# Mean of the last tokens ahead of the last quarter of the columns, by a column of summed weights in the last projection

## The chip, the cores and the metric

The kernel runs on one core of one Trainium2 chip. Five engines work side by side and are held together by semaphores: PE (TensorE, matrix products, with its weight load PEld), DVE (VectorE), ACT (ScalarE), POOL (GpSimd) and SP (SyncE), whose queue issues every DMA of this kernel. The metric is the device time of one execution in microseconds, lower is better; times are compared as medians of several runs.

## The reference

Two gated attention layers with a LayerNorm behind each, on 256 tokens of 1024 features. What matters here is the end of the second layer: the gated attention output `o * silu(gate)` is projected by `moba_w_o`, a scaled residual is added, and each token (a row) is normalized over its 1024 columns.

```
def layer_norm(x, g, b):
    xf = x.astype(jnp.float32)
    mu = jnp.mean(xf, axis=-1, keepdims=True)
    var = jnp.mean(jnp.square(xf - mu), axis=-1, keepdims=True)
    return ((xf - mu) * lax.rsqrt(var + LN_EPS) * g + b).astype(x.dtype)
...
def moba_mixer(x, k_blocks, v_blocks, k_mean, w_in, w_o, cos, sin):
...
    return (o * jax.nn.silu(gate)) @ w_o
...
        x = layer_norm(ALPHA * x + y, ln_g[layer], ln_b[layer])
    return x
```

The mean `mu` of a row is needed before the first subtraction, the variance before the multiplication by its inverse root.

## The kernel before

Tokens stand in two tiles of 128 (tok 0 and tok 1), features in eight chunks of 128. Every product of two float32 matrices is done in three matmuls: each operand is split into a high part in the reduced type fp32r and a low part, the rest (`split`: ACT casts the high part at line 376, DVE or POOL subtracts it from the source at line 387), and `passes` (line 406 in the profile) multiplies high by high, high by low and low by high into one PSUM bank.

Weights come in units of 128 x 1024, one DMA each, in the order of a list. A unit lands in one of five `raw` buffers, and its two parts go into one of six `wh` and six `wl` buffers; the last two units of the projections `oa`, `vb` and `ob` go into `x_h` and `x_l` instead. So the weights of the last projection, `ob`, eight units of one feature chunk by all 1024 columns, are split while the second attention layer still runs.

`token_products` runs a projection of tokens: for tok 0, one unit after the other over the columns 0 to 511 and 512 to 1023; tok 1 follows eight units later. With `last` given (only for `ob`), tok 1 goes through the eight units three times, for the columns 0 to 511, 512 to 767 and 768 to 1023, each in a PSUM bank of its own, and `last_b` is called when a bank is complete. It adds the scaled residual (`m` in the profile, `x1[1]` in the code), takes `bn_stats` of each 256 columns (line 918), and, after the last quarter, joins them with `bn_aggr` to mean and variance (line 924, in `mv`). POOL raises the variance to the power -0.5 (line 387, `mv<-mv,mhalf`). Then there are two steps for each quarter of 256 columns, both at line 391: the first, `act_h<-m,mv,lng`, subtracts the mean and multiplies by the gain, the second, `act_h<-act_h,mv,lnb`, multiplies by the inverse root and adds the bias; `act_h` is here the output row. Three DMAs write the output of tok 1.

The first layer's normalization (`layer_norm`, lines 807 and 808) is done for tok 0 and tok 1 in turn, on tiles of 512 columns; its result `m` is transposed by PE (line 420, `pt`), split into `act_h` and `act_l`, and projected by `vb`.

In the second attention layer, per head pair: scores into the banks `s`, DVE masks them and takes the minimum (line 713), ACT exponentiates and sums (line 380, `e`), DVE takes the reciprocal (line 719), POOL or DVE scales (line 400), PE transposes (`pt`), ACT copies the transposed tile (line 376), PE multiplies by the values (`pv`). Meanwhile PE computes projections of gates, queries and keys for later heads as filler.

The order of instructions on each engine isn't the order of the code: `Schedule` collects all operations with an estimated duration and their dependencies, and emits them by a priority list over the five engines. An engine takes its instructions strictly in the order in which they were emitted.

Of the kernel before, what the change touches and what calls it, by code (L numbers as in the profile page):

```python
# [8 lines left out]
F32R = mybir.dt.float32r  # L9
# [4 lines left out]
P = 128  # L14
# [329 lines left out]
def trunk(ctx, tc, W0, xtok, W, gq, gkv, lng, lnb, cosa, sina, coska, sinka, cosb, sinb, maskd, identd, out):  # L344
# [93 lines left out]
    raws = {}  # L438

# [14 lines left out]
    def weights(name, k):  # L454
        u = U[name, k]
        while state["hl"] <= u:
# [5 lines left out]
            if nm == "kr":  # L462
                hl = sc.val(wp, [P, 1024], F32R, "wh", HL_BUFS).rearrange("p (a b c) -> p a b c", b=2, c=64)
                r = raws.pop(v)[:, 0:n].rearrange("p (a c) -> p a c", c=64)
                split(hl[:, :, 0, :].at(0), hl[:, :, 1, :].at(1), r, n)
                hls[v] = hl.rearrange("p a b c -> p a (b c)")
                state["hl"] += 1
                continue
            if nm in ("oa", "vb", "ob") and kk >= 6:
                if kk == 6:  # L470
                    extra["h"] = C([P, 2, 1024], "x_h", F32R)
                    extra["l"] = C([P, 2, 1024], "x_l", F32R)
# [48 lines left out]
    def token_products(name, nk, lhs, tags, lag, done, last=None):  # L521
        banks = [None, None]
        n1 = nk * (3 if last else 1)
        for i in range(max(nk, n1 + lag)):
            for tok in range(2):
# [8 lines left out]
                if tok and last:  # L534
                    parts = (((0, 512), (512, 768), (768, 1024))[j // nk],)
                for c0, c1 in parts:
                    h, l = wsl(w, c0, c1)
                    ah, al = lhs(k, tok)
                    o = banks[tok][j // nk if tok and last else c0 // 512][:, 0:c1 - c0]
                    passes(o, ah, al, h, l, k == 0, k == nk - 1, c1 - c0)  # L540
                if tok and last:
                    if k == nk - 1:
                        last(o, c0, c1)
# [368 lines left out]
    st4, mv4 = C([P, 4, 6], "bst4"), C([P, 4], "mv4")  # L912

    def last_b(o, c0, c1):
        z = x1[1]
        stt(z[:, c0:c1].at(c0), z[:, c0:c1].at(None), ALPHA, o, ALU.mult, ALU.add, c1 - c0)
# [5 lines left out]
        if c1 < D:  # L922
            return
        sc.op("dve", 80, lambda: nc.vector.bn_aggr(A(mv4[:, 0:2]), A(st4)), [st4], [mv4.at(0)])
        tt(mv4[:, 2:3].at(1), mv4[:, 1:2].at(0), mhalf, ALU.pow, 5, "pool")
        y = C([P, 2, D], "act_h")[:, 0]

        def step(a, b, one):
            zi, yo = z[:, a:b].at(max(k for k in (0, 512, 768) if k <= a)), y[:, a:b].at(a // S)
            if one:  # L930
                stt(yo, zi, mv4[:, 0:1].at(0), gb[:, a:b], ALU.subtract, ALU.mult, b - a)
            else:
                stt(yo, yo, mv4[:, 2:3].at(1), bb[:, a:b], ALU.mult, ALU.add, b - a)

        for q in range(3):
            step(q * S, q * S + S, True)
        for q in range(2):
            step(q * S, q * S + S, False)
        dma(out[1][:, 0:512], y[:, 0:512], 2048 * P, r=[y.at(0), y.at(1)])
        step(768, 1024, True)  # L940
        for q in (2, 3):
            step(q * S, q * S + S, False)
            dma(out[1][:, q * S:q * S + S], y[:, q * S:q * S + S], 1024 * P, r=[y.at(q)])
# [94 lines left out]
```

## Time and profile before

| | us |
|---|---|
| median of three runs | 282.68 |
| lowest and highest run | 281.94 and 285.47 |
| the profiled execution | 284.01 |
| its span, first to last instruction | 282.2 |

The profiled execution has 1.81 us around its span, and stands 1.33 us above the median. Its TensorE clock was granted at 0.979 on average; it is 1.00 from 222 to 256 us. Times below are counted from the start of the span. In a row of the timeline stand the start, the duration, the engine, the line, the operation, its output and inputs with their shapes, the number of instructions merged in the row, and in brackets the idle time ahead of it with what ended it. SPq is the queue of SP. Duration means from start to end of one instruction; on ACT and DVE the next one can start some 0.1 us before the end of the one in front of it where it needn't wait for it.

### The profile page before, as it was taken

The numbers are of one execution on the slowest core, as the hardware profiler recorded it, in microseconds if no ns is written. First come the engines' busy times: TensorE is split into PE (matmuls) and PEld (weight loads), VectorE is DVE, ScalarE is ACT, GpSimd is POOL, SyncE is SP. The second block draws the span as 40 slices with busy tenths as digits, with TensorE's granted clock in tenths as the row PEclk, the third lists the DMA queues.
The fourth block names the chain that finished last, engine by engine and source line by source line (L and its number), as shares of the span: only waits on it lengthen the run. The fifth ranks groups of instructions, "written<-read, shape, count | busy, mean of one in ns | idle before, by whom it ended". The sixth has DMA issues, their size and how long they took to land.

```text
span 282.2 us, 5363 instructions
## 1 busy us (share of the span) xinstructions
PE 269.2 (95%) x1948; PEld 246.6 (87%) x1948; DVE 209.0 (74%) x450; ACT 159.6 (57%) x330; POOL 57.0 (20%) x72
## 2 busy tenths in 40 slices
PE   7799989999999999999999999999999999999990
PEld 4799989989989999878877889999999999887880
DVE  2557779989988767655998546868988979685655
ACT  3537769567695768822505744546855858692000
POOL 2000042400040034201010000522324445421100
PEclk9599999999999999999999999999999999999996
DMA  7897865766262442262288784465848768430012
GB/s 266 271 328 271 291 222 181 272 224 217 89 215 75 153 149 75 77 223 74 81 293 268 291 282 165 148 209 161 296 119 322 204 224 310 104 113 2 0 74 74
DMA packets 18537, 52.31 MB, mean 185 GB/s; under 512 B 2896, under 2 KB 6096, under 8 KB 18512
## 3 DMA queue, kind: packets, MB, share of 16 engines
q1 hardware_dynamic: 18512, 51.98, 54.8%
q8 instruction: 15, 0.25, 0.3%
q14 instruction: 10, 0.08, 0.1%
HBM read 45.68 MB, written 1.05 MB: 166 GB/s over the span
## 4 chain that ended last, share of the span: by engine, by line
PE 79%; issue 12%; DVE 5%; ACT 1%; POOL 1%; DMA 0%; SPq 0%; DVEq 0%; ACTq 0%
PE proj L406 58%; PE s L406 11%; PE pv L406 6%; PE pt L420 4%; DVE wl L387 2%; DVE m L391 1%; DVE act_h L391 1%; ACT wh L376 1%; DVE bst L807 0%; DMA raw<-in_W 0%; POOL mv L387 0%; POOL rk L387 0%; SPq L368 0%; DVE act_l L387 0%; ACT act_h L376 0%
## 5 line engine op out<-in xcount | busy, mean ns | idle before, releaser
L387 DVE TENSOR_TENSOR wl<-raw,wh 128x1024 fp32r<-128x1024 f32 (+2 forms) x74 | 87.2, 1187 | 22.0 <-ACT wh L376 20.3
L376 ACT CAST wh<-raw 128x1024 fp32r<-128x1024 f32 (+2 forms) x75 | 74.7, 1003 | 33.8 <-PE proj L406 14.9
L406 PE MATMUL proj<-act_h,wh 128*128 128x256 f32 x280 | 79.1, 283 | 0.0
L406 PE MATMUL proj<-act_h,wl 128*128 128x256 f32 x280 | 78.2, 279 | 0.0
L406 PE MATMUL proj<-act_l,wh 128*128 128x256 f32 x280 | 78.2, 279 | 0.0
L406 PEld LDWEIGHTS proj<-act_l,wh 128*128 128x128 f32 x280 | 52.6, 188 | 0.0
L406 PEld LDWEIGHTS proj<-act_h,wh 128*128 128x128 f32 x280 | 52.6, 188 | 0.0
L406 PEld LDWEIGHTS proj<-act_h,wl 128*128 128x128 f32 x280 | 52.5, 188 | 0.0
L380 ACT ACTIVATE e<-e,st 128x256 f32<-128x256 f32 x64 | 28.6, 451 | 8.0 <-DVE st L713 7.7
L400 POOL TENSOR_SCALAR e<-e,st 128x256 f32<-128x256 f32 (+1 forms) x32 | 16.1, 520 | 48.8 <-DVE st L719 48.7
L406 PE MATMUL s<-kq 128*128 128x256 f32 (+1 forms) x100 | 18.9, 316 | 0.4 <-DVE wl L387 0.4
L406 PE MATMUL proj<-x_h,wh 128*128 128x256 f32 x64 | 18.5, 289 | 0.0
L406 PE MATMUL proj<-x_h,wl 128*128 128x256 f32 x64 | 17.9, 279 | 0.0
L406 PE MATMUL proj<-x_l,wh 128*128 128x256 f32 x64 | 17.9, 279 | 0.0
L387 DVE TENSOR_TENSOR x_l<-raw,x_h 128x256 fp32r<-128x256 f32 (+1 forms) x14 | 10.4, 764 | 9.7 <-ACT x_h L376 9.7
L406 PEld LDWEIGHTS s<-kq 128*128 128x128 f32 x100 | 15.6, 190 | 1.9 <-PE pt L420 0.6
L376 ACT COPY pt<-pt 128x384 f32<-128x384 f32 x32 | 14.9, 474 | 3.5 <-PE pt L420 3.4
L376 ACT CAST x_h<-raw 128x256 fp32r<-128x256 f32 (+1 forms) x14 | 9.5, 685 | 11.3 <-DMA raw<-in_W 11.3
L420 PE MATMUL pt<-ident,e 128*128 128x128 f32 x96 | 15.1, 275 | 0.0
L387 POOL TENSOR_TENSOR t<-t,t512b 128x512 f32<-128x512 f32 x5 | 6.9, 1371 | 31.6 <-DVE t512b L387 17.5
L713 DVE CUSTOM_DVE_ANT_0 e<-s,masks,sca 128x256 f32<-128x256 f32 (+1 forms) x32 | 11.9, 412 | 1.8 <-PE pt L420 0.7
L387 POOL TENSOR_TENSOR mv<-mv,mhalf 128x1 f32<-128x1 f32 x4 | 3.5, 871 | 44.5 <-DVE mv L398 36.2
(166 smaller groups left out, 577.3 us busy)
## 6 DMA issues: line engine op xcount, KB each, us to landing
raw<-in_W SPq DMA_DIRECT2D x66, 512.0 KB, 4.3
raw<-in_W SPq DMA_DIRECT2D x7, 640.0 KB, 7.8
kq<-x_h SPq DMA_DIRECT2D x24, 96.0 KB, 2.2
raw<-in_W SPq DMA_DIRECT2D x5, 384.0 KB, 3.9
kq<-x_h SPq DMA_DIRECT2D x24, 64.0 KB, 2.0
lng<-in_lng SPq DMA_DIRECT2D x2, 512.0 KB, 4.1
lnb<-in_lnb SPq DMA_DIRECT2D x2, 512.0 KB, 5.3
raw<-in_xtok SPq DMA_DIRECT2D x2, 512.0 KB, 3.5
```

What stands on the lines that cost most here:

```text
L376: nc.scalar.copy(A(o), A(i))
L380: nc.scalar.activation(A(o), A(i), func, bias=A(bias), scale=A(scale), accum_out=A(accum))
L387: sc.op(eng, dur, lambda: e.tensor_tensor(A(o), A(a), A(b), op=op), [a, b], [o], lock=not (is_ps(a) or is_ps(b)))
L391: sc.op("dve", dur, lambda: nc.vector.scalar_tensor_tensor(A(o), A(a), A(s), A(b), op0=op0, op1=op1), [a, s, b], [o], lock=not (is_ps(a) o ...
L400: fn = lambda: e.tensor_scalar(A(o), A(a), A(s1), s2, op0=op0, op1=op1)
L406: nc.tensor.matmul(A(out_), A(lt), A(rh), start=st, stop=sp_, skip_group_check=True)
L420: nc.tensor.transpose(A(x), A(y), A(ident))
L713: nc.vector.tensor_tensor_reduce(A(e[:, cs]), A(ps[:, cs]), A(msk), scale=A(scale[b]), scalar=3.0e38, op0=ALU.add, op1=ALU.min, accum_out= ...
```

## The change

A product's mean over the columns is the product with the mean over the columns of the weights. The change uses this for the last quarter of `ob`. For each of the eight `ob` units, ACT sums the columns 768 to 1023 of the raw weights (one pass over 256 columns with an accumulator, into `wsum`), and the sum is split into a high and a low part, too, and written twice, as two extra columns behind the third quarter. For that, a unit's parts are kept as four quarters at a distance of 272 columns in buffers of 1088 columns. The second of the three turns of tok 1 is 258 columns wide instead of 256, so that its bank holds, in column 256, the sum over the last quarter of the projection before that quarter is computed.

The residual's part of the sum, `ms[:, 0:1]`, is taken by one more accumulating pass of ACT over `x1[1]` when the first layer's normalization has produced it. When the second bank is complete, the mean of the whole row is put together in `ms[:, 3:4]` from `bn_aggr` of three quarters and these sums, and the first step of the three quarters 0 to 2 is emitted there, ahead of the last bank. Behind the last bank stand `bn_stats`, `bn_aggr` of all four quarters (for the variance), the power on POOL, the first step of the last quarter and the second step of all four. The three DMAs of the output are the same in size; the first follows the second quarter.

The core of the diff:

```
+    wsum = C([P, 8], "wsum")
...
-                h = sc.val(wp, [P, 1024], F32R, "wh", HL_BUFS)[:, :]
-                l = sc.val(wp, [P, 1024], F32R, "wl", HL_BUFS)[:, :]
+                h = sc.val(wp, [P, 1088], F32R, "wh", HL_BUFS)[:, :]
+                l = sc.val(wp, [P, 1088], F32R, "wl", HL_BUFS)[:, :]
             r = raws.pop(v)
+            if nm == "ob":
+
+                h, l = (t.at((kk, 0)).rearrange("p (a b) -> p a b", b=272) for t in (h, l))
+                split(h[:, :, 0:S], l[:, :, 0:S], r[:, 0:n].at(0).rearrange("p (a b) -> p a b", b=S), n, eng=on("w", nm, kk))
+                act(T([P, S], "scr", 1), r[:, 768:n].at(0), S, AF.Identity, accum=wsum[:, kk:kk + 1].at(kk))
+                split(h[:, 2, S:S + 2], l[:, 2, S:S + 2], wsum[:, kk:kk + 1].at(kk).bc([P, 2]), 2)
+                hls[v] = (h, l, kk, "ob")
+                state["hl"] += 1
+                continue
...
+        if early == "ob":
+            if c1 - c0 == S + 2:
+                return h[:, c0 // S, 0:S + 2], l[:, c0 // S, 0:S + 2]
+            return h[:, c0 // S:c1 // S, 0:S], l[:, c0 // S:c1 // S, 0:S]
...
-                    parts = (((0, 512), (512, 768), (768, 1024))[j // nk],)
+                    parts = (((0, 512), (512, 770), (768, 1024))[j // nk],)
...
-    st4, mv4 = C([P, 4, 6], "bst4"), C([P, 4], "mv4")
-
-    def last_b(o, c0, c1):
+    st4, mv4, ms = C([P, 4, 6], "bst4"), C([P, 4], "mv4"), C([P, 4], "ms")
+    act(T([P, S], "scr", 1), x1[1][:, 768:D].at(None), S, AF.Identity, scale=ALPHA / D, accum=ms[:, 0:1].at(0))
+    y = C([P, 2, D], "act_h")[:, 0]
+
+    def last_b(bk, c0, c1):
         z = x1[1]
-        stt(z[:, c0:c1].at(c0), z[:, c0:c1].at(None), ALPHA, o, ALU.mult, ALU.add, c1 - c0)
...
+        stt(z[:, c0:c1].at(c0), z[:, c0:c1].at(None), ALPHA, bk[:, 0:c1 - c0], ALU.mult, ALU.add, c1 - c0)
+        if c0 == 512:
+            stt(ms[:, 1:2].at(1), bk[:, S:S + 1], 1.0 / D, ms[:, 0:1].at(0), ALU.mult, ALU.add, 1)
...
+        elif c0 == 512:
+            sc.op("dve", 80, lambda: nc.vector.bn_aggr(A(mv4[:, 0:2]), A(st4[:, 0:3, :])), [st4.at(q) for q in range(3)], [mv4.at(0)])
+            stt(ms[:, 3:4].at(3), mv4[:, 0:1].at(0), 0.75, ms[:, 1:2].at(1), ALU.mult, ALU.add, 1)
+            for q in range(3):
+                step(q * S, q * S + S, True)
+        else:
+            sc.op("dve", 80, lambda: nc.vector.bn_aggr(A(mv4[:, 0:2]), A(st4)), [st4], [mv4.at(0)])
+            tt(mv4[:, 2:3].at(1), mv4[:, 1:2].at(0), mhalf, ALU.pow, 5, "pool")
+            step(768, 1024, True)
+            for q in range(4):
+                step(q * S, q * S + S, False)
+                if q:
+                    a = 0 if q == 1 else q * S
+                    dma(out[1][:, a:q * S + S], y[:, a:q * S + S], (q * S + S - a) * 4 * P, r=[y.at(i) for i in range(a // S, q + 1)])
```

What this does to the order is seen at three places. The first is the end of DVE's queue, where `s` and the later `proj` are the second and third bank of tok 1, `m_1733` is its row and `bst`, `mv` hold its statistics. Before:

```order
L391 SCALAR_TENSOR_TENSOR m_1733<-m_1733,s 128x256
L918 BN_STATS bst_3329<-m_1733 128x6
L391 SCALAR_TENSOR_TENSOR m_1733<-m_1733,proj 128x256
L918 BN_STATS bst_3329<-m_1733 128x6
L924 BN_AGGR mv_3371<-bst_3329 128x2
L391 SCALAR_TENSOR_TENSOR act_h<-m_1733,mv_3371,lng 128x256 x3
L391 SCALAR_TENSOR_TENSOR act_h<-act_h,mv_3371,lnb 128x256 x2
L391 SCALAR_TENSOR_TENSOR act_h<-m_1733,mv_3371,lng 128x256
L391 SCALAR_TENSOR_TENSOR act_h<-act_h,mv_3371,lnb 128x256 x2
```

The same place on DVE after the change, with `ms` for the sums and the mean:

```order
L391 SCALAR_TENSOR_TENSOR m_1733<-m_1733,s 128x256
L391 SCALAR_TENSOR_TENSOR ms<-s,ms 128x1
L946 BN_STATS bst_3365<-m_1733 128x6
L951 BN_AGGR mv_3391<-bst_3365 128x2
L391 SCALAR_TENSOR_TENSOR ms<-mv_3391,ms 128x1
L391 SCALAR_TENSOR_TENSOR act_h<-m_1733,ms,lng 128x256 x3
L391 SCALAR_TENSOR_TENSOR m_1733<-m_1733,proj 128x256
L946 BN_STATS bst_3365<-m_1733 128x6
L956 BN_AGGR mv_3391<-bst_3365 128x2
L391 SCALAR_TENSOR_TENSOR act_h<-m_1733,ms,lng 128x256
L391 SCALAR_TENSOR_TENSOR act_h<-act_h,mv_3391,lnb 128x256 x4
```

Three of the four first steps moved from behind the third bank to ahead of it, with three small instructions new in front of them.

The second place is ACT's queue where the first layer's tok 1 has been normalized: the two `act_h` rows are the casts of its two transposed halves, and the `wh` row between them is a weight unit of the projection `vb`.

```order
 L376 CAST wh<-raw 128x1024
 L376 CAST act_h<-pt 128x4x128
+L380 ACTIVATE scr,ms<-m_1733 128x256
 L376 CAST wh<-raw 128x1024
 L376 CAST act_h<-pt 128x4x128
```

The pass over the residual was put between the first half's cast and the weight unit's.

The third place is ACT's queue in the second attention layer, at the casts of the gated attention output `oa` of two head pairs and the exponentials of the next two tiles of scores (the four `e,st` rows). Before:

```order
L376 CAST big_h<-oa 128x256 x2
L376 COPY pt<-pt 128x384
L380 ACTIVATE e,st<-e,st 128x256
L380 ACTIVATE e,st<-e,st 128x128
L380 ACTIVATE e,st<-e,st 128x256
L380 ACTIVATE e,st<-e,st 128x128
L378 ACTIVATE t_3002<-proj 128x256
L376 CAST wh<-raw 128x1024
```

The same place on ACT after the change:

```order
L376 CAST big_h<-oa 128x256 x2
L376 COPY pt<-pt 128x384
L380 ACTIVATE scr,wsum<-raw 128x256 x2
L380 ACTIVATE e,st<-e,st 128x256
L380 ACTIVATE e,st<-e,st 128x128
L380 ACTIVATE e,st<-e,st 128x256
L380 ACTIVATE e,st<-e,st 128x128
L378 ACTIVATE t_3018<-proj 128x256
L376 CAST wh<-raw 128x4x256
L376 CAST wh<-wsum 128x2
```

Two passes over weights stand ahead of the exponentials, and a cast of two columns behind the unit's cast. PE's order changes only here: the transposes of the second of these two tiles stand 3 instead of 9 filler matmuls behind the next scores, the scores after that move behind `pv`, and the transposes and scores behind them trade places with a few filler matmuls. SP and POOL keep their order.

More of the change, by code (lines that the diff above doesn't have):

```diff
@@ L462, in weights @@
             if nm == "kr":
-                hl = sc.val(wp, [P, 1024], F32R, "wh", HL_BUFS).rearrange("p (a b c) -> p a b c", b=2, c=64)
+                hl = sc.val(wp, [P, 1088], F32R, "wh", HL_BUFS)[:, 0:1024].rearrange("p (a b c) -> p a b c", b=2, c=64)
                 r = raws.pop(v)[:, 0:n].rearrange("p (a c) -> p a c", c=64)
@@ L539, in token_products @@
                     o = banks[tok][j // nk if tok and last else c0 // 512][:, 0:c1 - c0]
+                    if last and (c1 - c0) % S == 0:
+                        o = o.rearrange("p (a b) -> p a b", b=S)
                     passes(o, ah, al, h, l, k == 0, k == nk - 1, c1 - c0)
@@ L542, in token_products @@
                     if k == nk - 1:
-                        last(o, c0, c1)
+                        last(banks[tok][j // nk], c0, c1 // S * S)
                 elif j == nk - 1:
@@ L909, in finish_b, with step @@
             dma(out[tok][:, cs], x1[tok][:, cs].at(hf), 2048 * P)
-    st4, mv4 = C([P, 4, 6], "bst4"), C([P, 4], "mv4")
-    def last_b(o, c0, c1):
+    st4, mv4, ms = C([P, 4, 6], "bst4"), C([P, 4], "mv4"), C([P, 4], "ms")
+    act(T([P, S], "scr", 1), x1[1][:, 768:D].at(None), S, AF.Identity, scale=ALPHA / D, accum=ms[:, 0:1].at(0))
+    y = C([P, 2, D], "act_h")[:, 0]
+    def last_b(bk, c0, c1):
         z = x1[1]
-        stt(z[:, c0:c1].at(c0), z[:, c0:c1].at(None), ALPHA, o, ALU.mult, ALU.add, c1 - c0)
+        def step(a, b, one):
+            zi, yo = z[:, a:b].at(max(k for k in (0, 512, 768) if k <= a)), y[:, a:b].at(a // S)
+            if one:
+                stt(yo, zi, ms[:, 3:4].at(3), gb[:, a:b], ALU.subtract, ALU.mult, b - a)
+            else:
+                stt(yo, yo, mv4[:, 2:3].at(1), bb[:, a:b], ALU.mult, ALU.add, b - a)
+        stt(z[:, c0:c1].at(c0), z[:, c0:c1].at(None), ALPHA, bk[:, 0:c1 - c0], ALU.mult, ALU.add, c1 - c0)
+        if c0 == 512:
+            stt(ms[:, 1:2].at(1), bk[:, S:S + 1], 1.0 / D, ms[:, 0:1].at(0), ALU.mult, ALU.add, 1)
         for q in range(c0 // S, c1 // S):
@@ L921, in last_b @@
             ts(st4[:, 0, 2:3].at(0), st4[:, 0, 2:3].at(0), D * LN_EPS, None, ALU.add, None, 1, "dve")
[L922 to L943, printed above, removed]
+        elif c0 == 512:
[3 more added lines that the diff above has]
+                step(q * S, q * S + S, True)
+        else:
+            sc.op("dve", 80, lambda: nc.vector.bn_aggr(A(mv4[:, 0:2]), A(st4)), [st4], [mv4.at(0)])
[6 more added lines that the diff above has]
+                    dma(out[1][:, a:q * S + S], y[:, a:q * S + S], (q * S + S - a) * 4 * P, r=[y.at(i) for i in range(a // S, q + 1)])
     token_products("ob", 8, lhs_of(ogh2, ogl2), (("proj", "proj"), ("s", "s", "proj")), LAG, finish_b, last_b)
```

4 lines of the change are left out of this document (2 added, 2 removed).

## The prediction

> **What bounds the kernel now.** I read the page's busy shares first, then the timeline of the end, then the waits around each place where the order puts new instructions.
>
> ```profile
> span 282.2 us, 5363 instructions
> PE 269.2 (95%) x1948; PEld 246.6 (87%) x1948; DVE 209.0 (74%) x450; ACT 159.6 (57%) x330; POOL 57.0 (20%) x72
> ```
>
> PE is busy for 95% of the span, so a gain can only come from where PE isn't working: the end. A loss comes from whatever makes PE wait. The timeline from the last matmul on:
>
> ```profile
> 274.31 0.28 PE L406 MATMUL proj<-x_h,big_l 128*128 128x256 f32 x1
> 274.63 0.42 DVE L391 SCALAR_TENSOR_TENSOR m<-m,proj 128x256 f32<-128x256 f32 x1 [1.96 <-PE proj L406]
> 275.09 0.43 DVE L918 BATCH_NORM_STATS2 bst<-m 128x6 f32<-128x256 f32 x1
> 275.55 0.27 DVE L924 BATCH_NORM_AGGREGATE mv<-bst 128x2 f32<-128x24 f32 x1
> 275.85 1.30 DVE L391 SCALAR_TENSOR_TENSOR act_h<-m,mv,lng 128x256 f32<-128x256 f32 x3
> 275.89 0.56 POOL L387 TENSOR_TENSOR mv<-mv,mhalf 128x1 f32<-128x1 f32 x1 [8.32 <-DVE mv L924]
> 277.07 0.87 DVE L391 SCALAR_TENSOR_TENSOR act_h<-act_h,mv,lnb 128x256 f32<-128x256 f32 x2
> 277.86 0.47 DVE L391 SCALAR_TENSOR_TENSOR act_h<-m,mv,lng 128x256 f32<-128x256 f32 x1
> 278.26 0.87 DVE L391 SCALAR_TENSOR_TENSOR act_h<-act_h,mv,lnb 128x256 f32<-128x256 f32 x2
> ...
> L368 SPq DMA_DIRECT2D out<-act_h x3: 332/333/405, 278.0 to 279.2; - x3
> ...
> out<-act_h SPq DMA_DIRECT2D x2, 128.0 KB, 1.9
> ```
>
> From 274.63 on DVE is never idle: residual, statistics, eight steps, done at 279.13. The last DMA is issued at 279.2, lands 1.9 us later, and the span ends at 282.2. Before 274.63 DVE sat idle for 1.96 us. Every step taken out of this queue is worth its pitch; POOL's power ends at 276.45 and nobody waits for it, because three first steps cover it.
>
> **The end, part by part.** Removed behind the third bank: three first steps. `bn_aggr` still ends at 275.82. The remaining first step no longer needs it, so it starts as a DVE instruction without a wait does, about 0.08 early (277.86 against 277.94), at 275.75, and ends at 276.22. Now the power loses its cover: the second steps wait for it. Its price has two rows, 0.56 above and this one, from the first layer's normalization:
>
> ```profile
> 144.89 0.74 DVE L391 SCALAR_TENSOR_TENSOR m<-m,mv,lng 128x512 f32<-128x512 f32 x1
> 145.05 1.00 POOL L387 TENSOR_TENSOR mv<-mv,mhalf 128x1 f32<-128x1 f32 x1 [11.38 <-DVE mv L398]
> 146.09 0.75 DVE L391 SCALAR_TENSOR_TENSOR m<-m,mv,lnb 128x512 f32<-128x512 f32 x1 [0.46 <-POOL mv L387]
> ```
>
> There the power began 0.16 behind the start of a DVE step, took 1.00, and ended 0.42 behind that step's end (146.05 against 145.63); in the old end it began 0.04 behind one and took 0.56. In the new end it begins at 275.89, 0.14 behind, so I take the slow form: 276.22 + 0.42 = 276.64, and DVE 0.04 later, 276.68. Four second steps follow: 3 x 0.40 + 0.47 = 1.67, done at 278.35 instead of 279.13, a gain of 0.78. With the fast form (276.45) it is 0.97. [...]
>
> The three DMAs are ready at 277.55, 277.95 and 278.35. At 0.33 to 0.41 per issue SP keeps up, so the last goes out 0.78 earlier, too. They come a little closer together, which I cost at nothing (bounds 0 and 0.3, from spreads of 1.2 before and 0.8 after): the landing of 1.9 covers the others' transfer.
>
> **Ahead of the third bank.** The moved work must fit before 274.63.
>
> ```profile
> 271.79 0.42 DVE L391 SCALAR_TENSOR_TENSOR m<-m,s 128x256 f32<-128x256 f32 x1 [1.20 <-PE s L406]
> 272.25 0.43 DVE L918 BATCH_NORM_STATS2 bst<-m 128x6 f32<-128x256 f32 x1
> ...
> L398 DVE TENSOR_SCALAR mv<-mv 128x1 f32<-128x1 f32 x3 | 0.5, 154 | 0.1
> ```
>
> Residual until 272.21, one column of `ms` (0.15, nearest row `mv`) until about 272.3, statistics until 272.75, `bn_aggr` 0.27, `ms` 0.15, three first steps 1.30, with hand-overs of 0.03: done between 274.5 and 274.6. It fits with about 0.1 to spare, so it costs 0; if the small ones cost double, 0.3 of the gain goes.
>
> PE's second turn is two columns wider: 24 matmuls at a pitch of 0.117 for 256 columns (274.31 is 0.117 behind its predecessor) give 24 x 2/256 x 0.117 = 0.02. The 72 matmuls of 512 columns now read the weights from two stretches instead of one. The nearest row is the scores', whose third matmul reads two stretches of keys:
>
> ```profile
> 244.59 0.52 PE L406 MATMUL s<-kq 128*128 128x256 f32 x3
> 244.94 0.28 PE L406 MATMUL proj<-act_h,wh 128*128 128x256 f32 x1
> ```
>
> Three in 0.35 is the plain pitch of 0.117, so I take 0; a hundredth for three, the rows' resolution, times 72 would be 0.2, the upper bound.
>
> **The pass over the residual, at 149 us.** This is the term that the diff hides. ACT, DVE and PE there:
>
> ```profile
> 148.37 0.59 ACT L376 CAST act_h<-pt 128x512 fp32r<-128x512 f32 x1 [7.05 <-PE pt L420]
> 148.85 1.05 ACT L376 CAST wh<-raw 128x1024 fp32r<-128x1024 f32 x1
> ...
> 149.80 0.59 ACT L376 CAST act_h<-pt 128x512 fp32r<-128x512 f32 x1
> ...
> 149.94 1.22 DVE L387 TENSOR_TENSOR wl<-raw,wh 128x1024 fp32r<-128x1024 f32 x1
> ...
> 151.08 0.68 DVE L387 TENSOR_TENSOR act_l<-pt,act_h 128x512 fp32r<-128x512 f32 x1
> ...
> 151.68 2.35 DVE L387 TENSOR_TENSOR x_l<-raw,x_h 128x1024 fp32r<-128x1024 f32 x2
> ...
> 153.08 0.39 PE L406 MATMUL proj<-x_l,act_h 128*128 128x512 f32 x1
> ```
>
> The `wl` at 149.94 waits for the cast that ends at 149.90; `act_l` and two `x_l` follow without a gap. The first `x_l` ends at 152.90, and PE reads it at 153.08: only 0.13 to spare with a hand-over of 0.05. The new pass goes ahead of the cast. What it takes is seen in the exponentials, the same form:
>
> ```profile
> 222.17 0.51 ACT L380 ACTIVATE e<-e,st 128x256 f32<-128x256 f32 x1
> 222.59 0.19 ACT L380 ACTIVATION_READ_ACCUMULATOR e<-e,st 128x1 f32 x1
> 222.68 0.39 ACT L380 ACTIVATE e<-e,st 128x128 f32<-128x128 f32 x1
> ```
>
> From 222.17 to 222.68, 0.51. So the cast, `wl`, `act_l` and `x_l` come 0.51 later, and PE waits 0.51 - 0.13 = 0.38. PE has no later idle time of its own from which to take it back (it computes in order, and what it waits for in the next layer hangs on its own results), so I charge all of it. Bounds: 0, if the order's slack is larger than these rows say, and 0.51. [...]
>
> **The passes over the weights.** Eight passes at 0.51, eight two-column casts (nearest row below), eight two-column subtractions on DVE (0.15 as `mv`, 1.2 together, in its idle time).
>
> ```profile
> L378 ACT ACTIVATE sca<-proj,eps 128x2 f32<-128x2 f32 x1 | 0.3, 256 | 0.0
> ...
> 236.40:256.40 20.00, 19.60 (x145) 17.55 (x144) 15.91 (x53) 15.09 (x42) 6.87 (x10) 1.00 0.41 115
> ...
> 237.27 0.51 ACT L380 ACTIVATE e<-e,st 128x256 f32<-128x256 f32 x1 [0.41 <-DVE st L713]
> ...
> 238.63 3.52 POOL L400 TENSOR_SCALAR e<-e,st 128x256 f32<-128x256 f32 x4 [1.33 <-DVE st L719]
> ...
> 242.06 0.59 PE L406 MATMUL s<-kq 128*128 128x256 f32 x3 [0.40 <-DVE wl L387]
> 242.49 0.28 PE L406 MATMUL proj<-act_h,wh 128*128 128x256 f32 x1
> ```
>
> From 236.40 to 256.40 ACT is busy for 15.09 of 20 us (the fourth busy time of the row); six passes and some six casts, 6 x 0.51 + 6 x 0.26 = 4.6, go there, nearly all of the 4.9 idle. Two passes stand ahead of the exponentials at 237.27. With 0.41 idle there and 1.02 new, these come about 0.5 later (two passes from 236.76). POOL's scaling, done at 242.15, would be done at about 242.7. The transposes that need it now stand three filler matmuls behind the scores: 242.49 + 3 x 0.12 = 242.85. It just fits, by 0.1. Behind it I followed each transposition and each copy in the new order in the same way and found 0.6 or more to spare. So I cost this at nothing; the cover is the filler matmuls, and if it is gone, each tile late by 0.5 costs PE up to that. Bounds 0 and 1.0, two such delays.
>
> **Sum.** -0.78 + 0.02 + 0.38 = -0.38. On the profiled execution, 284.01 (1.81 around its span of 282.2), that gives 283.6, span 281.8. That execution is 1.33 above the median of the runs; from the median, 282.68, the forecast is 282.3.
>
> **Rivals.** First, the whole gain: PE doesn't wait at 153, or wins it back. For it: the spare of 0.13 is a difference of rows that vary by some hundredths; against it: DVE's four instructions stand back to back. It gives 282.68 - 0.76 = 281.9, and 281.7 with the fast power.
>
> Second, slower: ACT becomes the bound of the second attention layer. One mechanism: the passes at 236.8 delay exponentials, the scaling and so the transposes at 242.85. It decides once PE waits more than 0.38 there; the price is 1.0 at full, 283.3. For it: 4.6 us put into 4.9 idle. Against it: PE's filler.
>
> Third, the change doesn't do what it says: the moved steps aren't through at 274.63 (the chain of small instructions costs 0.3 each instead of 0.15) and hold the residual of the last bank up, and the DMAs' bunching takes 0.3. Then 0.6 of the gain goes, 282.9. Against it: the small rows are 0.15 each time.
>
> **How the numbers follow.** Forecast 0.45, first rival 0.2, second 0.2, third 0.1, none of these 0.05. The range takes in all three rivals, from 281.7 less some 0.4 for the runs' scatter (their lowest is 0.7 below the median) to 283.3 and 0.4: 281.3 to 283.7. 2%, about what a measurement of this kernel can tell from no change, is 5.7 us; no case comes near. Faster by that 0.01, slower 0.02, the rest within.
>
> **What would show it.** In the changed profile: three first steps ending by 274.6 + 0.4 with DVE idle or just free at the last residual; between the last matmul's end and the last `lnb` 0.8 less than 4.5; POOL's power at about 0.75 (0.56 is the fast form); PE with an idle of 0.3 to 0.4 at `proj<-x_l` near 153.5, released by DVE `x_l`; and between 236 and 258 no wait of PE above 0.5. Wrong would be: waits of PE on POOL `e` or ACT `pt` there, or a wider pitch of the matmuls that read the weights in quarters.

## The result, and the profile after

| | kernel before | changed kernel |
|---|---|---|
| median, first session (22 runs each) | 283.0 | 285.62 |
| lowest and highest | 279.51 and 285.47 | 282.21 and 289.66 |
| ratio, 95% interval | | 1.0107 (1.0081 to 1.0133) |
| ratio in a second session (12 runs against 29) | | 1.0049 (1.0022 to 1.0076) |
| profiled execution, its span | 284.01, 282.2 | 283.29, 281.1 |

Medians are over all runs, while the ratios leave out, on both sides, runs more than 1.5% above the fastest of the same kernel. The changed kernel is slower by 0.5 to 1.1%, 1.6 to 2.6 us, and not 0.4 us faster. The three runs of before that the prediction started from stood low: over all sessions the medians of the kernel before lie between 283.0 and 284.3.

The two profiled executions can't be compared by their spans. These are the page's rows of the granted clock, before and then after, in 40 slices of some 7 us:

```profile
PEclk9599999999999999999999999999999999999996
```

```profile
PEclk9999999999999999999999999999999999999997
```

Before had the clock at half (0.50) for 6.8 us near its start: from 8.80 us on, the starts of 24 matmuls spread over 5.81 us there, and those of the same 24 over 3.21 in after, which had the clock in full (1.00) until its matmuls were done. Such half windows stand ahead of the last matmul in 12 of the 20 profiles of this study, at changing places. So below I compare stretches between two matmuls with the same place in PE's order; where a half window lies in between, the text says so.

The end, in the timeline of the changed kernel:

```profile
272.79 1.27 DVE L391 SCALAR_TENSOR_TENSOR act_h<-m,ms,lng 128x256 f32<-128x256 f32 x3
274.24 0.42 DVE L391 SCALAR_TENSOR_TENSOR m<-m,proj 128x256 f32<-128x256 f32 x1 [0.18 <-PE proj L406]
274.70 0.43 DVE L946 BATCH_NORM_STATS2 bst<-m 128x6 f32<-128x256 f32 x1
275.16 0.26 DVE L956 BATCH_NORM_AGGREGATE mv<-bst 128x2 f32<-128x24 f32 x1
275.34 0.42 DVE L391 SCALAR_TENSOR_TENSOR act_h<-m,ms,lng 128x256 f32<-128x256 f32 x1
275.50 0.67 POOL L387 TENSOR_TENSOR mv<-mv,mhalf 128x1 f32<-128x1 f32 x1 [8.33 <-DVE mv L956]
276.20 1.67 DVE L391 SCALAR_TENSOR_TENSOR act_h<-act_h,mv,lnb 128x256 f32<-128x256 f32 x4 [0.45 <-POOL mv L387]
277.11 1.31 SPq L368 DMA_DIRECT2D out<-act_h  x3
```

The three first steps end at 274.06, 0.18 us ahead of the last residual: the moved work fits. Behind it stand one first step, 0.45 us of idle while DVE waits for POOL's power (0.67), and four second steps, which end at 277.87. From the start of the last matmul to the end of the span it is 7.18 us; before it was 7.88. The gain of the end is there: 0.70. On DVE alone it is 0.87 (from the last residual's start to the last step's end 3.63 us instead of 4.50); the rest goes behind the last step, where the last of the three DMAs, now closer together, is issued some 0.1 later and takes some 0.1 more to land.

The pass over the residual, at 146 us, ACT and PE:

```profile
146.15 0.42 ACT L380 ACTIVATE scr<-m 128x256 f32<-128x256 f32 x1
146.47 0.19 ACT L380 ACTIVATION_READ_ACCUMULATOR scr<-m 128x1 f32 x1
146.56 1.04 ACT L376 CAST wh<-raw 128x1024 fp32r<-128x1024 f32 x1
...
150.27 0.40 PE L406 MATMUL proj<-x_h,act_h 128*128 128x512 f32 x1
150.65 0.50 PE L406 MATMUL proj<-x_l,act_h 128*128 128x512 f32 x1
150.98 0.40 PE L406 MATMUL proj<-x_h,act_l 128*128 128x512 f32 x1
```

From pass to cast it is 0.41 us. The first matmul with `x_l` starts 0.38 behind the one with `x_h`, where the pitch is 0.23: a wait of 0.15, and 0.33 instead of 0.23 once more behind it.

The attention of the second layer, around the transposes that wait longest. Changed kernel, timelines of POOL, DVE and PE:

```profile
241.43 0.55 PE L420 MATMUL pt<-ident,e 128*128 128x128 f32 x3 [0.31 <-POOL e L400]
...
247.24 1.88 POOL L400 TENSOR_SCALAR e<-e,st 128x256 f32<-128x256 f32 x2 [2.30 <-DVE st L735]
247.74 1.22 DVE L387 TENSOR_TENSOR wl<-raw,wh 128x1024 fp32r<-128x1024 f32 x1
249.17 0.55 PE L420 MATMUL pt<-ident,e 128*128 128x128 f32 x3 [0.59 <-POOL e L400]
```

Before, the same places:

```profile
246.24 1.22 DVE L387 TENSOR_TENSOR wl<-raw,wh 128x1024 fp32r<-128x1024 f32 x1
247.70 0.83 POOL L400 TENSOR_SCALAR e<-e,st 128x256 f32<-128x256 f32 x2 [2.03 <-DVE st L719]
249.00 0.49 PE L420 MATMUL pt<-ident,e 128*128 128x128 f32 x3
```

In the changed order DVE's low part of a weight unit (`wl`, 1.22) starts in the middle of POOL's two scalings, and they take 1.88 instead of 0.83; PE waits 0.59. Before, `wl` was over at 247.46, and the scaling began at 247.70. The kernel before has the slow form elsewhere: the four scalings of 3.52 from 238.63 on, which the prediction shows, would be 1.66 at this pace, and on DVE two `wl` run beside them:

```profile
238.37 1.21 DVE L387 TENSOR_TENSOR wl<-raw,wh 128x1024 fp32r<-128x1024 f32 x1
...
240.67 1.25 DVE L387 TENSOR_TENSOR wl<-raw,wh 128x1024 fp32r<-128x1024 f32 x1 [0.51 <-ACT wh L376]
```

The wait at 241.43 is the one that the prediction held covered by 0.1.

Last, a row far from anything that the diff touches: the 280 matmuls of 256 columns with `act_l` and `wh`, from the pages of before and after (total, mean ns of one):

```profile
L406 PE MATMUL proj<-act_l,wh 128*128 128x256 f32 x280 | 78.2, 279 | 0.0
```

```profile
L406 PE MATMUL proj<-act_l,wh 128*128 128x256 f32 x280 | 79.1, 283 | 0.0
```

One takes 4 ns longer, in stages that begin over 100 us ahead of the change's first instruction (146.15). With its two sister groups these are 840 matmuls.

### The profile page after: what moved, and what is told of

It reads as the page before. It is cut to its first block, busy times and chain, and to the rows that moved or that the text cites. A ratio compares the mean times of both kernels' runs of the same rounds, so it can differ in the third digit from the quotient of the medians.

```text
span 281.1 us, 5393 instructions
## 1 busy us (share of the span) xinstructions
PE 269.2 (96%) x1948; PEld 246.7 (88%) x1948; DVE 210.1 (75%) x461; ACT 163.8 (58%) x356; POOL 57.0 (20%) x72
## 3 DMA queue, kind: packets, MB, share of 16 engines
HBM read 45.68 MB, written 1.05 MB: 166 GB/s over the span
## 4 chain that ended last, share of the span: by engine, by line
PE 74%; issue 14%; DVE 5%; POOL 3%; ACT 1%; DMA 0%; SPq 0%; POOLq 0%; DVEq 0%; ACTq 0%
PE proj L406 56%; PE s L406 8%; PE pv L406 6%; PE pt L420 4%; POOL e L400 2%; DVE wl L387 2%; DVE m L391 1%; DVE bst L823 1%; POOL mv L387 1%; DVE act_h L391 0%; ACT wh L376 0%; DMA raw<-in_W 0%; ACT e L380 0%; POOL rk L387 0%; SPq L368 0%
## 5 line engine op out<-in xcount | busy, mean ns | idle before, releaser
L406 PE MATMUL proj<-act_h,wh 128*128 128x256 f32 x280 | 80.1, 286 | 0.0
L406 PE MATMUL proj<-act_h,wl 128*128 128x256 f32 x280 | 79.1, 283 | 0.0
L406 PE MATMUL proj<-act_l,wh 128*128 128x256 f32 x280 | 79.1, 283 | 0.0
L406 PEld LDWEIGHTS proj<-act_l,wh 128*128 128x128 f32 x280 | 53.6, 191 | 0.0
L406 PEld LDWEIGHTS proj<-act_h,wh 128*128 128x128 f32 x280 | 53.5, 191 | 0.0
L406 PEld LDWEIGHTS proj<-act_h,wl 128*128 128x128 f32 x280 | 53.5, 191 | 0.0
L400 POOL TENSOR_SCALAR e<-e,st 128x256 f32<-128x256 f32 (+1 forms) x32 | 17.1, 548 | 50.0 <-DVE st L735 48.1
L420 PEld LDWEIGHTS pt<-ident,e 128*128 128x128 f32 x96 | 11.1, 140 | 2.5 <-POOL e L400 1.5
```

The lines of the kernel that those rows point to most:

```text
L400: fn = lambda: e.tensor_scalar(A(o), A(a), A(s1), s2, op0=op0, op1=op1)
L406: nc.tensor.matmul(A(out_), A(lt), A(rh), start=st, stop=sp_, skip_group_check=True)
L420: nc.tensor.transpose(A(x), A(y), A(ident))
```

## Experiments

Each kernel ran against the kernel before on the same chip. The following table gives what I read from the traces: the time from the start of one matmul to another's, counted by place in PE's order. A: 741 matmuls of the first layer, from about 39 us on. B: the next 46, with the first layer's last `x_l`. C: the next 300. D: from the scores near 224 us to the start of the last matmul. E: from there to the end of the span. F: time around the span, median over the runs.

| kernel | A | B | C | D | E | F | ratio (95% interval) |
|---|---|---|---|---|---|---|---|
| before | 104.52 | 10.46 | 40.17 | 49.50 | 7.88 | 1.79 | |
| before, run again | 104.50 | 10.46 | 40.17 | 50.10 | 7.87 | 1.80 | 0.9983 (0.9950 to 1.0017) |
| wide1088 | 104.50 | 10.46 | 40.17 | 50.43 | 7.89 | 1.80 | 0.9985 (0.9954 to 1.0016) |
| before_plus32 | 104.89 | 10.48 | 39.94 | 50.02 | 7.87 | 1.80 | 0.9986 (0.9954 to 1.0019) |
| before_plus64 | 104.99 | 10.52 | 40.55 | 49.91 | 7.87 | 1.79 | 1.0020 (0.9975 to 1.0066) |
| before_plus96 | 104.73 | 10.47 | 40.33 | 50.56 | 7.88 | 1.78 | 1.0027 (0.9982 to 1.0071) |
| code_on_dve | 104.52 | 10.46 | 40.18 | 50.55 | 7.86 | 1.78 | 0.9946 (0.9905 to 0.9987) |
| code_on_act | 104.44 | 10.48 | 40.19 | 49.36 | 7.87 | 1.77 | 0.9973 (0.9928 to 1.0018) |
| tail_only | 104.50 | 10.47 | 40.17 | 50.54 | 7.18 | 1.77 | 1.0009 (0.9971 to 1.0047) |
| changed | 104.97 | 10.80 | 40.54 | 50.72 | 7.18 | 2.16 | 1.0107 (1.0081 to 1.0133) |
| changed, run again | 104.97 | 10.79 | 40.55 | 51.52 | 7.18 | 2.12 | 1.0049 (1.0022 to 1.0076) |
| sums_mean_late | 104.97 | 10.79 | 40.55 | 50.96 | 7.88 | 2.01 | 1.0121 (1.0076 to 1.0167) |
| after_pad128 | 103.93 | 10.83 | 40.09 | (51.82) | 7.18 | 2.15 | 1.0005 (0.9963 to 1.0046) |
| after_residual_late | 103.89 | 10.55 | 40.09 | (53.66) | 7.19 | 2.14 | 1.0088 (1.0042 to 1.0133) |
| passes_twice | 104.31 | 10.81 | 39.94 | 51.19 | 7.19 | 2.00 | 1.0015 (0.9968 to 1.0061) |
| after_wl_moved | 104.42 | 10.81 | 39.94 | 50.83 | 7.19 | 2.16 | 1.0007 (0.9970 to 1.0045) |
| sums_in_the_casts | 103.93 | 10.54 | 39.95 | 51.79 | 7.19 | 1.97 | 0.9981 (0.9934 to 1.0028) |
| sums_in_casts_wl_moved | 104.27 | 10.53 | 40.09 | 51.11 | 7.18 | 1.94 | 0.9981 (0.9943 to 1.0018) |
| after_order_of_before | 104.41 | 10.81 | 40.09 | 50.30 | 7.19 | 1.80 | 0.9964 (0.9923 to 1.0004) |
| sums_in_casts_order_of_before | 103.97 | 10.55 | 40.09 | 50.17 | 7.18 | 2.14 | 0.9931 (0.9885 to 0.9976) |

The two values in brackets have a half window of the clock (3.4 us at half) in them. In after_pad128 it begins where D begins, and its first 16 matmuls, to the start of the 17th, take 3.40 us where they take 1.85 in before: 1.55 us lost. The busy times of PE, PEld, DVE, ACT and POOL in it, then the granted clock:

```profile
225.00:228.40 3.40, 3.40 (x18) 3.40 (x18) 2.66 (x11) 2.27 (x8) 1.04 (x3) 0.50 0.42 102
```

Without these 1.55, D is by estimate 50.3 there. B and E repeat to some hundredths from run to run, and so do A and C where addresses are alike and lie as before or 64 bytes on; at 128 bytes on, A spreads over 0.5. D varies by 0.5 and more, because it holds waits for DMAs of keys (0.6 us in r_before, 1.8 in sums_in_the_casts).

One part of D, which I call G, has no wait for a DMA in any kernel, and a half window only in after_residual_late: from the scores that the prediction shows at 242.06 to the start of the 91st matmul behind them. The same matmuls stand in it in every order. G takes 12.81 to 12.95 us in the nine kernels with the order of before, and 14.27, 13.74, 14.07 and 13.69 in the changed kernel, its repeat, sums_mean_late and after_pad128: 0.8 to 1.4 more, 1.06 on average.

### Both kernels again

> The kernel before, unchanged, for a profile and clocks of the same chip as the others. Two theories of the 1.07% that the change lost. Buffers: the weight buffers of 1088 columns instead of 1024 slow the matmuls that load weights from them (0.118 us apart before, 0.120 after in the two profiles, over about a thousand of them, some 2 us). Queues: ACT's added passes make PE wait (0.15 at 151 us, 0.31 and 0.59 at the transposes) and the rest is scatter between chips and starts. Both expect a ratio of 1.000 here; the buffers' theory expects a pitch of 0.118 on this chip, too; if it is 0.120 here, the pitch is the chip's.

> The changed kernel on the same chip. Both theories expect about 1.010. Buffers: pitch of the 256-column matmuls 0.120 where the kernel before has 0.118. Queues: the same pitch in both, and the waits of PE together over 2 us.

The kernel before repeats within its interval. The changed one is slower again, by less than in the first session, and its wait at the transposes near 250 us is the same 0.59. What the records show in A and C repeats to 0.02.

### The width of the buffers alone

`wide1088` is the kernel before with its weight buffers 1088 columns wide, order unchanged (`[P, 1024]` to `[P, 1088]` at `wh`, `wl`, `x_h` and `x_l`).

> The kernel before with nothing changed but the size of the weight buffers, 1088 columns instead of 1024, of which 1024 are used; every engine has the same instructions in the same order. Buffers: slower by 2 us or more, ratio 1.007 to 1.012, pitch 0.120. Queues: the same as before, ratio 1.000 within 0.002.

A, B and C are those of before: the width does nothing.

### The sums without the moved end

`sums_mean_late` keeps all sums of the changed kernel, but the first steps and the mean stand behind the last bank as before.

```
-        elif c0 == 512:
...
-            for q in range(3):
-                step(q * S, q * S + S, True)
+        if c1 < D:
+            return
...
+        for q in range(3):
+            step(q * S, q * S + S, True)
```

> The changed kernel with all sums, extra columns and wide buffers, but with the mean and all first steps behind the last bank as before. Both theories expect it slower than the changed kernel by the tail's gain, 0.7 us in the two profiles: 1.012 to 1.014 against the kernel before.

E is 7.88 again, A to C and the wider pitch are those of the changed kernel. Neither theory had the reason for A and C, which the order of instructions cannot give. What is left is where the buffers lie: the change adds two tiles, `ms` and `wsum`, 32 bytes per partition each, ahead of all weight buffers.

### Addresses

Three kernels are before with one tile, `mv4`, made longer, and the fourth is the changed kernel with `ms` made longer. No instruction moves.

```
-    st4, mv4 = C([P, 4, 6], "bst4"), C([P, 4], "mv4")
+    st4, mv4 = C([P, 4, 6], "bst4"), C([P, 24], "mv4")
```

> The kernel before with one small tile, mv4, 64 bytes per partition longer, so that all weight buffers and the working tiles behind it lie 64 bytes further on, as in the changed kernel (wh at byte 138784, 32 above a multiple of 128; before 138720, 96 above one). The order of all instructions is that of before. Theory Address: the pitch of the 256-column projection matmuls goes from 0.118 to 0.120 us between 45 and 240 us; over some 1000 of them that is 2 us, ratio to before 1.004 to 1.009. Rival Program: the pitch comes from what the changed kernel executes (its added passes, its order), so the pitch stays 0.118 and the ratio is 0.998 to 1.002.

> The kernel before with the same tile 32 bytes longer, so that the weight buffers start at multiples of 128 bytes (wh at 138752); order as before. Theory Address: if what counts is how rows of the weights lie against lines of 64 or 128 bytes, full alignment is at least as good as before: pitch 0.116 to 0.118, ratio 0.990 to 1.000. Rival Program: pitch 0.118, ratio 0.998 to 1.002.

> The same, 96 bytes longer (wh at 138816, 64 above a multiple of 128). Theory Address with lines of 64 bytes: as plus32. With lines of 128 bytes: between the others, pitch 0.118 to 0.120, ratio 0.995 to 1.008. Rival Program: pitch 0.118, ratio 0.998 to 1.002.

> The changed kernel with its tile ms 80 bytes longer, so that the buffers behind the new tiles lie a multiple of 128 bytes further on than before (wh at byte 139872, 96 above a multiple of 128, as before); order as in the changed kernel. Theory Address: pitch back at 0.118, ratio to before 1.000 to 1.005 (what is left is 0.9 us of waits of the transposes and -0.7 at the end), ratio to the changed kernel near 0.993. Rival Program: pitch 0.120, ratio to before 1.007 to 1.013 as the changed kernel.

The same group of matmuls, from the pages of before_plus64 and then of after_pad128:

```profile
L406 PE MATMUL proj<-act_l,wh 128*128 128x256 f32 x280 | 79.1, 283 | 0.0
```

```profile
L406 PE MATMUL proj<-act_l,wh 128*128 128x256 f32 x280 | 78.3, 280 | 0.0
```

64 bytes alone give the changed kernel's row and its A (104.99 against 104.97) and C (40.55); 128 bytes take both away. So a shift of 64 bytes costs 0.47 in A, 0.06 in B and 0.38 in C, 0.9 in 155 us, and it is most of what the changed kernel loses there, and about half of the 2 us that the theory gave. 32 and 96 bytes lie between in the sum of the three (0.2 and 0.4). Wrong was my guess that full alignment is best: at a multiple of 128 bytes (plus32), A is 0.4 longer than before, though C is 0.2 shorter. Which operand it is (weights, or the working tiles behind them, which move alike) these runs don't tell, and the earlier and later stages can't be read for it. The times agree, but don't decide: 1.0020 has 1 in its interval, and the interval of after_pad128 lies below the first session's of the changed kernel and overlaps the second's.

### The end alone

```
+        elif c0 == 512:
+            sc.op("dve", 80, lambda: nc.vector.bn_aggr(A(mv4[:, 0:2]), A(st4[:, 0:3, :])), [st4.at(q) for q in range(3)], [mv4.at(0)])
+            ts(ms[:, 3:4].at(3), mv4[:, 0:1].at(0), 0.75, None, ALU.mult, None, 1, "dve")
+            for q in range(3):
+                step(q * S, q * S + S, True)
```

> The kernel before with the changed end alone: the first step of three quarters moved ahead of the last bank, the DMAs' order as changed, the new scalar kept inside the 32 bytes that mv4 already has, so that no address moves. No sums over weights or residual, so the last quarter's part of the mean is left out. Theory Three terms (the end gains, the passes on ACT make PE wait, the addresses widen the pitch): last matmul to end of span 6.8 to 6.95 us (before 7.57), ratio to before 0.995 to 0.999, pitch 0.118. The time around the span, 1.80 in every variant of before and 2.13 in the changed kernel: 1.80 if the extra 0.33 comes with the added instructions, 2.0 to 2.15 if with the new end. Rival Scatter (outside of addresses the change is worth nothing that can be found): 0.998 to 1.002.

E is 7.18, a gain of 0.70 with nothing else moved, as expected (6.8 to 6.95 behind the last matmul is 7.1 to 7.3 from its start). F is 1.77, so the new end alone doesn't lengthen the time around the span. In the runs the gain doesn't stand out: 282.61 against 283.22 by medians, but a ratio of 1.0009, above the expected 0.995 to 0.999, with 1 in its interval.

### The pass over the residual

```
     act(T([P, S], "scr", 1), x1[1][:, 768:D].at(None), S, AF.Identity, scale=ALPHA / D, accum=ms[:, 0:1].at(0))
+    sc.ops[-1].preds[cast_of["gb", 1]] = True
```

> The padded changed kernel (buffers 128 bytes on) with the pass over the residual held behind a weight cast near 182 us, where ACT idles 1.8 us per cast; all else in the order of the changed kernel. Three terms: the stretch of 46 matmuls around the first layer's last x_l (150 us) takes 10.46 to 10.52 us again instead of 10.80; 0.3 us less in all, ratio to before 0.999 to 1.004. Scatter: the stretch keeps 10.7 to 10.8, since the stall has another cause.

B falls from 10.83 to 10.55, just above the expected 10.46 to 10.52: the pass costs 0.28. The ratio, 1.0088, lies outside the expected 0.999 to 1.004. Its trace shows waits of PE on POOL `e` of 2.6 us in all, 1.63 of it at the transposes ahead of the scores near 240 us, and the half window right behind; why its runs were slower than those of after_pad128 (285.05 against 284.84 by medians, but against a faster kernel before, 283.22 against 283.91) isn't settled.

### Is ACT the bound?

```
-                act(T([P, S], "scr", 1), r[:, 768:n].at(0), S, AF.Identity, accum=wsum[:, kk:kk + 1].at(kk))
+                for _ in range(2):
+                    act(T([P, S], "scr", 1), r[:, 768:n].at(0), S, AF.Identity, accum=wsum[:, kk:kk + 1].at(kk))
```

> The padded changed kernel with each of the eight passes over the weights done twice, 8 x 0.41 = 3.3 us more on ACT between 222 and 258 us. Three terms: ACT has only some 0.3 us free there, so the exponentials, POOL's scaling and the transposes come later still: PE's waits on POOL e, ACT pt or DVE wl between 236 and 258 us grow by 1 to 3 us, ratio to before 1.005 to 1.014. Scatter (passes hidden behind PE): growth below 0.5 us, ratio 0.998 to 1.004.

In the PE timeline the transposes ahead of the scores wait for POOL:

```profile
242.24 0.55 PE L420 MATMUL pt<-ident,e 128*128 128x128 f32 x3 [1.71 <-POOL e L400]
```

PE's waits between 236 and 258 us are 2.0 us in all, 1.8 of it on POOL; in after_pad128 they are 1.25, of it 0.66 on POOL and 0.59 on a DMA of keys. D is 51.19 against 50.3 without the half window. So some growth came, at the lower end of the expected 1 to 3 us or below it. But the runs don't show it (1.0015 against 1.0005), G is shorter than in after_pad128 (13.12), the planner had put the instructions in yet another order, and the same transposes wait 1.63 in after_residual_late, where no pass is done twice. This run doesn't decide what ACT's added time costs.

### The sums in the casts

If the cast accumulates as it goes, the passes should be nearly free.

```
-                split(h[:, :, 0:S], l[:, :, 0:S], r[:, 0:n].at(0).rearrange("p (a b) -> p a b", b=S), n, eng=on("w", nm, kk))
-                act(T([P, S], "scr", 1), r[:, 768:n].at(0), S, AF.Identity, accum=wsum[:, kk:kk + 1].at(kk))
+                act(h[:, :, 0:S], r4, n, AF.Identity, accum=wsum[:, kk:kk + 1].at(kk))
+                tt(l[:, :, 0:S], r4, h[:, :, 0:S].f32(), ALU.subtract, n, on("w", nm, kk))
```

> The changed kernel without separate passes over the weights: the cast of each of the eight last units to its high part accumulates the whole row of 1024 columns as it goes (one read of the accumulator more, 0.1 us, instead of 0.41), so the extra column holds the sum of all columns and the mean needs no statistics of three quarters; the residual's pass covers all 1024 columns and is held near 182 us; buffers 128 bytes on. Three terms: 2.6 us less on ACT between 222 and 258 us, PE's waits on POOL e there at most 0.3 in all; no stall at 150 us; end as in the changed kernel; ratio to before 0.995 to 1.000, to the changed kernel 0.985 to 0.992. Scatter: as the padded changed kernel, 0.998 to 1.004.

The ratio is within its range (0.9981), but not told apart from the kernel before. PE still waits 0.85 in all for POOL at the transposes, where at most 0.3 was expected, and 1.78 for a DMA of keys, which is why D is long.

### One instruction moved

```
         self.out = self.order()
+        v = {t: x for (_, t), x in self.tags.items()}
+        a, b = v["wl"][70].ops[0], v["G"][15].ops[0]
+        self.out.remove(a)
+        self.out.insert(self.out.index(b) + 1, a)
```

> The padded changed kernel (buffers 128 bytes on) with a single instruction moved on VectorE, by hand in the finished order: the low part of the fifth last unit of weights (1.22 us) stands two places later, behind the reciprocal and the gate that it stood ahead of, so it no longer runs beside POOL's scaling. All other engines keep their order. Theory Beside: POOL's two scalings take 0.8 to 1.0 us instead of 1.88, PE's wait at the transposes near 249 to 252 us (0.66) goes to 0 to 0.1, the stretch from there to the last matmul is 0.5 to 0.7 shorter, ratio to before 0.998 to 1.003. Rival Late (the exponentials come late from ACT): scaling and wait stay within 0.2.

> The version with the sums in the casts, the residual's pass at 182 us and buffers 128 bytes on, with the same instruction moved. Beside: the wait there (0.32) goes, ratio to before 0.994 to 0.999. Late: as without the move, wait 0.2 to 0.4.

The timelines of POOL and PE in after_wl_moved, four lines of code later than in the changed kernel:

```profile
249.14 0.83 POOL L404 TENSOR_SCALAR e<-e,st 128x256 f32<-128x256 f32 x2 [2.27 <-DVE st L739]
...
253.61 0.52 PE L424 MATMUL pt<-ident,e 128*128 128x128 f32 x3 [0.40 <-DVE e L404]
```

The scalings take 0.83 again and nobody waits for them: that `wl` stood beside them was the cause, as the first theory had it. But DVE is late now where `wl` went, and the next transposes wait 0.40 for DVE's own scaling. In sums_in_casts_wl_moved it is the same (0.41). Of 0.66, 0.26 is won; a stall went one place on. The expected 0.5 to 0.7 on the stretch didn't come: G is 13.96 against 13.69, with a wait of 0.31 at its first transposes that after_pad128 hasn't.

### Two attempts at the time around the span

`code_on_dve` and `code_on_act` add ten and twenty idle instructions to the kernel before.

> The kernel before with ten clears of one column on VectorE while it idles near 257 us: nothing but instructions. If the time around the span hangs on VectorE's instructions (559 before, 568 in the changed kernel), the instruction queue shows 11 packets and the time around the span 1.97 to 2.16 instead of 1.79; else 10 packets and 1.77 to 1.82.

> The kernel before with twenty copies of one column on ScalarE behind its last work, while it idles near 260 us. If it hangs on ScalarE's instructions, 11 packets and 1.97 to 2.16 around the span; else 10 packets and 1.77 to 1.82.

Both stayed at 1.77 to 1.78 around the span, code_on_act with 11 packets of instructions, so neither the count of instructions nor that of packets explains the 1.94 to 2.16 of the changed kernels.

### The old order with the added work

The added work enters the planner's durations as zero, so that PE's instructions stand as before (and in the second kernel the sums are in the casts, and the residual's pass is late).

```
+                for o in sc.ops[-3:]:
+                    o.dur = 0
...
-                    passes(o, ah, al, h, l, k == 0, k == nk - 1, c1 - c0)
+                    passes(o, ah, al, h, l, k == 0, k == nk - 1, (c1 - c0) // S * S)
```

> The padded changed kernel (buffers 128 bytes on), with the added passes, casts and subtractions entered in the planner's durations as zero, so that PE's instructions stand in exactly the order of before; ACT still carries the passes between them (8 x 0.41 us, and 8 x 0.09). If the planner's new order made PE wait: the stretch from the scores at 241 us to the last matmul is 33.0 to 33.5 us again (changed order: 33.9 to 34.2), ratio to before 0.998 to 1.003. If ACT's added time does it: 34.0 or more, PE waits on POOL e, DVE e or ACT pt of 0.6 to 1.5, ratio 1.002 to 1.008.

> The version with the sums in the casts and the residual's pass at 182 us, with the added work entered as zero in the planner, so that PE's order is that of before. Both theories: the stretch 32.9 to 33.5 us, no stall at 150 us, the end 0.7 us shorter than before, some 0.15 more around the span; ratio to before 0.995 to 0.999, to the changed kernel 0.985 to 0.992.

D is 50.30 and 50.17, inside the 49.4 to 50.6 of the nine kernels with the old order, with all of ACT's passes in the first of them. G, the cleaner measure, is 13.24 and 12.87, against 12.81 to 12.95 in those nine and 1.06 more in the changed order. So with all of ACT's passes, but in the old order, 0.36 of the 1.06 is left, and without the passes nothing. The waits that are left of 0.15 and more, in the PE timelines of the first and then of the second:

```profile
242.42 0.55 PE L420 MATMUL pt<-ident,e 128*128 128x128 f32 x3 [1.12 <-POOL e L400]
```

```profile
236.50 0.55 PE L420 MATMUL pt<-ident,e 128*128 128x128 f32 x3 [0.49 <-POOL e L400]
237.71 0.59 PE L406 MATMUL s<-kq 128*128 128x256 f32 x3 [0.66 <-DMA kq<-x_h]
```

They stand ahead of G, where the nine kernels of the old order wait, too: 0 to 0.55 at these transposes and 0.23 to 1.00 at the scores behind them (0.40 in the kernel before, quoted in the prediction). The 1.12 is a wait of the size that the theory of ACT's added time gave; it is longer than any at these transposes in the nine, but here the scores behind don't wait, and D is no longer for it. The transposes inside G don't wait. The first kernel is level with before or better (0.9964); the second has the lowest ratio of the study, 0.9931 (0.9885 to 0.9976), and is ahead of the changed kernel (282.71 against 285.62 by medians, in other sessions). That it beats the kernel before is not shown: by the medians of all runs it is 282.71 against 283.03, a ratio of 0.999, and the first kernel is ahead of it (282.18). And code_on_dve, which can gain nothing, came out at 0.9946 with 1 outside its interval, too, so such an interval proves little here. The second kernel's trace has the end 0.70 shorter and 0.35 more around the span, which leaves some 0.3.

## Why the prediction was wrong

**The end** (-0.78): right. 0.70, in the trace of every kernel that has it; the power came in its slow form, 0.67, and the second steps began at 276.20, 1.96 behind the last residual's start, where the working gave 2.05. The gain on DVE was so 0.87; 0.17 of it went behind the last step, where the prediction cost the closer DMAs at nothing, with 0.3 as a bound.

**Ahead of the third bank** (0): right, with 0.18 to spare instead of 0.1. **Columns and stretches** (+0.02 and 0): right; second turn 2.86 us for 24 matmuls in the changed kernel against 2.84 in before_plus64, and the 512-column matmuls at 0.234 and 0.233.

**The pass over the residual** (+0.38): right in place, mechanism and sign; it measured 0.28, because the pass takes 0.41 and not the exponentials' 0.51.

**The weights' passes** (0): this is the step that failed. "Behind it I followed each transposition and each copy in the new order in the same way and found 0.6 or more to spare" used durations from the old order, and POOL's 0.83 for two scalings was one from a place with no `wl` of DVE beside it (begun at 247.70, when `wl` was over at 247.46). In the new order it was 1.88, 1.05 more, against a spare that was put at 0.6 or more. The price stood in a row that the prediction quotes, four scalings of the kernel before in 3.52. The first spare, 0.1 at the transposes behind the scores, was gone, too, in the profile of the changed kernel (PE waited 0.31), though not in its repeat, where the scores came 0.70 later for a DMA. The prediction had two times of POOL beside DVE's steps, 0.56 and 1.00, at the power, where little hung on it, and did not ask for them at the scaling, where it decided. The price: waits of 0.6 to 0.7 at the transposes near 249 us in all five kernels with this order, and by G 0.8 to 1.4 for all that the new order and the passes cost there. after_wl_moved shows the cause of the slow scalings, and that the wait mostly moves on. The second rival had the sign and the place, and its price of 1.0 is near what was measured, but ACT's added time is the smaller part: with the same passes in the old order 0.36 of the 1.06 is left (after_order_of_before). The larger part is the order that the planner made of it.

**Not in the sum at all**: the addresses, +0.9, shown by 64 bytes alone; and +0.35 around the span, measured and not explained (the new end alone has 1.77, the added instructions in the old order 1.80). after_order_of_before has the same instructions as after_pad128 in another order and 1.80 against 2.15.

Together: -0.70 + 0.28 + 0.9 + 0.35 + 0.8 to 1.4 = 1.6 to 2.2, against 1.6 to 2.6 measured. And 0.3 or more of the miss is the base, a median of three runs.

## What to carry to other kernels

When a planner orders the work, a few added microseconds on an engine with room cost what the new order makes of them: follow the new neighbours of each instruction on the path, not only its due time, above all where POOL and DVE can meet (two scalings of POOL took 0.83 us here, and 1.88 with a `wl` of DVE beside them). Before an edit that adds a tile is judged, pad the tile so that everything behind it moves by 128 bytes; here 64 bytes cost 0.9 us, more than the edit could gain, and with 128 A was 103.89 to 104.42 and C 39.94 to 40.09 (104.52 and 40.17 before). (Kernels padded alike by 128 bytes still differed by up to 0.5 in A, which is open.) Before two stretches are compared, look where the half windows of the clock lie in each (1.55 us in D of after_pad128). To add side work to a tuned order, enter it at no cost in the plan, keep the order, and look for the waits that come.

## What the runs showed of the hardware

- The place of SBUF buffers changes the matmuls' pace without any instruction moving: from 175 to 200 us, 256-column matmuls stand 0.118 us from start to start in the mean with `wh` at 96 bytes above a multiple of 128, and 0.120 at 32 above (before and before_plus64). At 128 bytes further on it is 0.117 to 0.118.
- Two scalings of POOL, 0.83 us, take 1.88 when a `wl<-raw,wh` of DVE of 1.22 us starts beside them (changed kernel, 247.24), which itself keeps its 1.22.
- An accumulating pass of ACT over 256 columns, to the next instruction's start, takes 0.41 us (changed kernel, 146.15); an accumulation within a cast costs one read more, 0.09 (sums_in_casts_order_of_before, 236.36 to 236.45).
- The clock was granted at half for 3.4 or 6.8 us at places that changed from run to run (near 8 us, at 34 us, at 225 and at 242 us). In the one near 8 us (before), 256-column matmuls stand 0.213 us apart, and 0.118 in the same place of the changed kernel; the one at 225 us (after_pad128) costs 1.55 us, and by estimate from its 5.81 us against 3.21 the one near 8 us costs 2.6. Over the 29 runs of the kernel before in r_before's session, time and mean granted clock go against each other (correlation -0.81), so this is much of the scatter of single runs.
- The four half windows between 30 us and the last matmul came right behind stretches in which PE had waited: PE was busy for 2.35 of 3.90 us ahead of 33.9 (changed, run again), 1.69 of 3.40 ahead of 34.5 (code_on_act), 1.43 of 3.50 ahead of 225.0 (after_pad128) and 1.73 of 3.70 ahead of 241.7 (after_residual_late). Not every such stretch was followed by one: passes_twice, busy for 1.82 of 3.40 us from 238.7 on, kept the full clock.
